# One pool of 4 KB tiles, and weight tiles that stay over several products, in a decoder trunk of fp32 matmuls

## The chip, the core and the metric

The kernel runs on one core of a Trainium2 chip. The metric is the device time of one execution in microseconds. A core has five engines that each work through a queue of their own, in order: TensorE (PE; its weight loads are listed apart as PEld), VectorE (DVE), ScalarE (ACT), GpSimd (POOL) and SyncE (SP). They wait for each other through semaphores. In this kernel SP issues nearly all plain loads from DRAM and the transposing DMAs, POOL issues the loads that add to what a tile holds, and all of them run on the core's 16 DMA engines.

## The reference, cut to what matters

Two layers over 512 positions of width 1024. Each layer is a half-weighted SwiGLU FFN, a token mixer (recurrent in layer 0, chunked spatial gating in layer 1) and a second FFN; a final RMSNorm ends it.

```python
def swiglu(x, w_in, w_out):                      # w_in 1024 x 5632, w_out 2816 x 1024
    g, u = jnp.split(x @ w_in, 2, axis=-1)
    return (jax.nn.silu(g) * u) @ w_out

for i in range(DEPTH):                           # DEPTH = 2
    h = h + 0.5 * swiglu(rms_norm(h, ffn1_norm[i]), ffn1_w_in[i], ffn1_w_out[i])
    m = recurrent_mixer(...) if i % 2 == 0 else spatial_gating_mixer(...)
    h = h + m
    h = h + 0.5 * swiglu(rms_norm(h, ffn2_norm[i]), ffn2_w_in[i], ffn2_w_out[i])
return rms_norm(h, final_norm)
```

All inputs are fp32. There are four FFNs; the change touches the output product (`@ w_out`) of the first three.

## The kernel before, in words

**Precision.** Every operand of a matmul is split into a high and a low part (`hi` by an ACT copy to the rounded type, `lo` by a DVE subtraction), and each product is three matmuls: hi·hi, lo·hi, hi·lo. The weights' parts are `whi` and `wlo`, four tiles each (pool `wp`).

**Seven products for eight.** A large product is cut into 2 x 2 blocks, A (activations) times B (weights), and done by seven block products (`seven`), in the order that the table CHAIN gives for the first three FFNs:

- P1 = A11·B11 and P2 = A12·B21
- P5 = S1·(B11+B12), P6 = S2·(B11+B12+B22), Q4 = A22·(B11+B12+B22+B21)
- P3 = S4·B22, P7 = S3·(B22+B12)

S1 to S4 are sums of blocks of A (DVE). In an output product the inner dimension of each block has six cuts: one of a single row of 128 (half a block, 256 KB) and five of two rows (512 KB). One product with one cut is a step, an entry of `subs`; a whole block's step has 12 matmuls of 128x512. CHAIN lists 42 steps: the six of P1, the six of P2, sixteen in which P5, P6 and the first four of Q4 take turns, and fourteen of P3, P7 and the last two of Q4.

**Raw weights.** `Raw` is a tile with a weight block as it is in DRAM. Its `load` issues the SP DMA (line 142), `add` the POOL DMA that adds another block to it (line 145). `Sub.split` makes whi (ACT, line 103) and wlo (DVE, line 94) from it; before that `Sub.add` may add another raw tile to it on DVE, and after the split `then` may add one more block by POOL. Of a block that is to become a sum right away (`plus`), the addition is put into POOL's queue some steps after the load (`pending`).

For one cut of an output product of the first three FFNs this gives, before the change: a load of B11 for P1 and one of B21 for P2; a second load of B11 and an addition of B12 for P5; a load of B22, which DVE adds to that tile for P6, and then an addition of B21 to it for Q4; a second load of B22 for P3, and after its split an addition of B12 for P7. That is five loads and three additions.

**The order of the work.** The program is written out step by step by the loop at the end of `trunk`; the scheduler keeps that order on each engine. At step i the loop runs the additions that are due, the hooks of phase "pre" (sums of blocks), the splits of the steps up to i+3 (`SPLIT_AHEAD`), the hooks of phases "mid" and "rest", then `load_more`, which loads raw tiles in the order of their use while fewer than `RAW_BUFS` = 8 are alive, and then the matmuls of step i. At the end of a product, DVE adds the result to the residual X (line 100), and the next norm squares it (ACT) and turns it by transposes on PE (lines 274 and 615) two or three steps later.

**Memory.** Raw tiles have a pool of their own, 8 tiles of 4 KB a partition. Everything else of this size (parts of A and their splits, partial results, planes) takes 2 KB slots from a pool of 60. A tile of a pool is free for reuse once all work on it is done, and the first write to it waits for that.

**Planes.** The result of an input product is turned into the left operand of the output product by DMA: `Group.cross` copies each tile into two planes of 16-bit halves (ACT), transposes them by DMA (SP), and merges them again (ACT, five and six steps later). `cross` handles two names (two blocks of A) at a time; both were copied and transposed in the same step, into two plane tiles and two result tiles of 2 KB.

Of the kernel before, what the change touches and what calls it, by code (L numbers as in the profile page):

```python
# [14 lines left out]
P = 128  # L15
# [17 lines left out]

RAW_BUFS = 8
SPLIT_AHEAD = 3
SLOTS = 60


KORDER = (0, 2, 4, 6, 1, 3, 5, 7)
# [20 lines left out]
def trunk(ctx: ExitStack, tc: tile.TileContext, a: dict, out: bass.AP):  # L60
    nc = tc.nc
    PS = bass.MemoryType.PSUM
    cp = ctx.enter_context(tc.tile_pool(name="cp", bufs=1))
    sp = ctx.enter_context(tc.tile_pool(name="sp", bufs=SLOTS))
    rawp = ctx.enter_context(tc.tile_pool(name="rawp", bufs=RAW_BUFS))
    wp = ctx.enter_context(tc.tile_pool(name="wp", bufs=4))
    tp = ctx.enter_context(tc.tile_pool(name="tp", bufs=8))
    mmp = ctx.enter_context(tc.tile_pool(name="mmp", bufs=6, space=PS))
# [1 line left out]
    ctx.enter_context(tc.manual_schedule())  # L70

    uid = [0]

    def nm(s):
        uid[0] += 1
        return f"{s}_{uid[0]}"

    def slot(dt=F32, name="s"):
        return sp.tile([P, T], dt, tag="s", name=nm(name))

    def bank(name="ps"):
        return mmp.tile([P, 512], F32, tag="mm", name=nm(name))
# [22 lines left out]
    def split(src):  # L105

        w = src.shape[-1]
        hi, lo = slot(F32R, "hi")[:, :w], slot(F32R, "lo")[:, :w]
        act(hi, src, AF.Copy)
        tt(lo, src, f32(hi), ALU.subtract)  # L110
        return hi, lo
# [1 line left out]

    live = set()
    pending = []
    now = [0]

    class Raw:

# [9 lines left out]

        def load(self):  # L130
            _, k, c = self.shape
            t = rawp.tile([P, 1024], F32, tag="raw", name=nm("raw"))
            self.v = t[:, : k * c].rearrange("p (k c) -> p k c", k=k)
            live.add(self)
            self.fetch()
            if self.plus is not None:
                pending.append((now[0] + self.wait, self))
                pending.sort(key=lambda p: p[0])
# [70 lines left out]
            assert self.sub.hi is not None  # L209

    raws = []

    def raw_of(src, shape, *plus):
        raws.append(Raw(src, shape, *plus))
# [40 lines left out]
    class Group:  # L255


        def __init__(self, n):
            self.n, self.f, self.hl, self.whole = n, {}, {}, False

        def new(self, name):
            self.f[name] = slot(name=name.lower())[:, : self.n * H]
            return self.f[name]

        def part(self, name, q):
# [28 lines left out]

        def direct(self, name, ps, gains):

            hi, lo = self.hl[name] = slot(F32R, "hi")[:, : self.n * H], slot(F32R, "lo")[:, : self.n * H]
            cs = [(slice(q * H, (q + 1) * H), g) for q, g in enumerate(gains)]
            for c, g in cs:
                act(hi[:, c], ps[:, c], AF.Copy, scale=g)  # L300
            for c, g in cs:
                stt(lo[:, c], ps[:, c], g, f32(hi[:, c]), ALU.mult, ALU.subtract)

        def cross(self, half, tiles, planes, merges, parts):

            w, names = 2 * self.n * P, ("A12", "A11") if half == 0 else ("S1", "A22")
            if half == 0:
                names = names[::-1]
            dt = {}

            def move():
                pl = [sp.tile([P, 2 * T], U16, tag="s", name=nm("pl"))[:, : 2 * w] for _ in tiles]
                for k, name in enumerate(names):
                    c = slice(k * w, (k + 1) * w)
                    d = dt[name] = sp.tile([P, 2 * T], U16, tag="s", name=nm("dt"))[:, : 2 * w]
                    v = d.rearrange("p (m s t) -> p m s t", s=2, t=P)
                    for s, (t, h) in enumerate(zip(pl, tiles)):
                        act(t[:, c].rearrange("p (b f) -> p b f", b=2),
                            h.bitcast(U16)[:, c].rearrange("p (f b) -> p b f", b=2), AF.Copy)
                        nc.sync.dma_start_transpose(out=v[:, :, s, :], in_=t[:, c])  # L320
                tiles.clear()
# [52 lines left out]
    def seven(block, cuts, left, w, posts, order=None, own=False, apart=False, joined=None, opening=None,  # L374
# [165 lines left out]
    class BlockNorm:  # L540


        def __init__(self, grow, plain=False, late=False, wait=()):


            self.g = [Group(2), Group(2)]
            self.grow, self.plain, self.late, self.wait = grow, plain, late, wait

        def src(self, i, name):
# [39 lines left out]
    class TileNorm:  # L589
# [29 lines left out]
        def take(self, half):  # L619
            for k in KORDER:  # L620
                ps = self.ps[k // 2][:, k % 2 * H : (k % 2 + 1) * H]
                if half == 0:
                    self.z[k] = (slot(F32R, "zh"), slot(F32R, "zl"))
# [26 lines left out]
    def out_blocks(w, k0, groups, scale, norm=None, order=None, own=False, soon={}, swap=False, p2_lag=0, chain=False):  # L650
# [934 lines left out]
    def part(i, name, q, vector=False):  # L1585

        g, c, gain = first.g[i], slice(q * H, (q + 1) * H), first.src(i, name)[1][q]
        if name not in g.hl:
            g.hl[name] = slot(F32R, "hi"), slot(F32R, "lo")
        hi, lo = (t[:, c] for t in g.hl[name])  # L1590
        src = opening[i, name][:, c]
        if vector:
# [106 lines left out]
```

## Time and profile before

| | us |
|---|---|
| median of three runs | 1603.8 (1600.93 to 1604.03) |
| the profiled execution | 1606.85 |
| its span | 1605.0 |
| PE busy in it | 1581.6 (99%) |
| DVE busy | 1315.6 (82%) |
| ACT busy | 1158.9 (72%) |

The mean granted clock of TensorE was 0.992. 275.84 MB were read from HBM.

How to read the lines: a timeline's row begins with the start and the length in us, then engine, line of the kernel, instruction, the tile written and the tiles read, shapes and the count; in brackets stands how long the engine was idle before it and what ended that. SPq, POOLq and ACTq are the queues that issue DMAs. In a table of waits a row tells who waited, for whom, how long in total, how often, and the longest of them. Matmuls are pipelined: a row of 0.39 us is followed by the next some 0.23 us later, so the pace is read from the starts.

### The profile page before, as it was taken

The numbers are of one execution on the slowest core, as the hardware profiler recorded it, in microseconds if no ns is written. First come the engines' busy times: TensorE is split into PE (matmuls) and PEld (weight loads), VectorE is DVE, ScalarE is ACT, GpSimd is POOL, SyncE is SP. The second block draws the span as 40 slices with busy tenths as digits, with TensorE's granted clock in tenths as the row PEclk, the third lists the DMA queues.
The fourth block names the chain that finished last, engine by engine and source line by source line (L and its number), as shares of the span: only waits on it lengthen the run. The fifth ranks groups of instructions, "written<-read, shape, count | busy, mean of one in ns | idle before, by whom it ended". The sixth has DMA issues, their size and how long they took to land.

```text
span 1605.0 us, 20741 instructions
## 1 busy us (share of the span) xinstructions
PE 1581.6 (99%) x7149; PEld 1304.4 (81%) x7149; DVE 1315.6 (82%) x1759; ACT 1158.9 (72%) x1696; POOL 222.5 (14%) x201
## 2 busy tenths in 40 slices
PE   9999999999999999999899999999999999999998
PEld 7788887788888888888788888887788888888886
DVE  6977777978998877778878777789878989889788
ACT  7877786558777777786567777865786775675676
POOL 2111103200010111102201111022211011111120
PEclk9999999999999999999999999999999999999999
DMA  8888779953283887779937888799888557796793
GB/s 292 182 189 192 186 213 245 202 138 97 87 213 103 178 205 193 182 222 240 209 99 182 190 193 186 211 253 200 218 199 209 158 124 194 181 221 172 174 225 100
DMA packets 247465, 299.24 MB, mean 186 GB/s; under 512 B 94672, under 2 KB 120384, under 8 KB 247360
## 3 DMA queue, kind: packets, MB, share of 16 engines
q1 hardware_dynamic: 197856, 204.78, 41.4%
q0 software_dynamic: 47712, 91.30, 33.9%
q10 hardware_dynamic: 1792, 1.84, 0.3%
q8 instruction: 56, 0.92, 0.2%
q14 instruction: 49, 0.40, 0.1%
HBM read 275.84 MB, written 2.10 MB: 173 GB/s over the span
## 4 chain that ended last, share of the span: by engine, by line
PE 79%; DMA 6%; issue 5%; DVE 4%; ACT 2%; POOL 1%; ACTq 0%; SPq 0%; POOLq 0%
PE A L421 12%; PE A L422 12%; PE A L423 12%; PE C L422 6%; PE C L423 6%; PE C L421 6%; DMA raw<-in_ffn_w_out_dram 6%; PE p L892 4%; PE B L421 3%; PE B L423 3%; PE B L422 3%; PE r L232 2%; PE r L234 2%; PE r L233 2%; PE e L274 1%
## 5 line engine op out<-in xcount | busy, mean ns | idle before, releaser
L94 DVE TENSOR_TENSOR wlo<-raw,whi 128x1024 fp32r<-128x1024 f32 (+1 forms) x537 | 639.0, 1192 | 230.6 <-ACT whi L103 228.6
L103 ACT ACTIVATE whi<-raw 128x1024 fp32r<-128x1024 f32 (+1 forms) x537 | 553.1, 1031 | 237.5 <-PE C L422 58.4
L421 PE MATMUL A<-whi,hi 128*128 128x512 f32 x1016 | 401.0, 395 | 1.9 <-ACT c L103 1.9
L422 PE MATMUL A<-whi,lo 128*128 128x512 f32 x1016 | 396.9, 391 | 0.0
L423 PE MATMUL A<-wlo,hi 128*128 128x512 f32 x1016 | 396.9, 391 | 0.0
L421 PEld LDWEIGHTS A<-whi,hi 128*128 128x128 f32 x1016 | 191.9, 189 | 46.7 <-ACT c L103 7.9
L423 PEld LDWEIGHTS A<-wlo,hi 128*128 128x128 f32 x1016 | 191.4, 188 | 40.6 <-DVE wlo L94 0.4
L422 PEld LDWEIGHTS A<-whi,lo 128*128 128x128 f32 x1016 | 191.8, 189 | 39.0 <-DVE lo L94 0.3
L422 PE MATMUL C<-whi,lo 128*128 128x512 f32 x560 | 218.9, 391 | 1.3 <-DVE lo L94 1.2
L421 PE MATMUL C<-whi,hi 128*128 128x512 f32 x560 | 218.2, 390 | 0.0
L423 PE MATMUL C<-wlo,hi 128*128 128x512 f32 x560 | 218.1, 389 | 0.0
L145 POOL DMA_DIRECT2D raw<-in_ffn_w_in_dram x82 | 99.1, 1215 | 731.4 <-ACT pl L103 312.2
L103 ACT ACTIVATE hi<-a 128x512 fp32r<-128x512 f32 (+1 forms) x188 | 111.6, 600 | 55.9 <-DVE a L94 54.3
L145 POOL DMA_DIRECT2D raw<-in_ffn_w_out_dram x72 | 83.3, 1196 | 367.4 <-DVE wlo L94 185.6
L94 DVE TENSOR_TENSOR raw<-raw,raw 128x1024 f32<-128x1024 f32 (+1 forms) x108 | 129.6, 1200 | 0.9
L422 PEld LDWEIGHTS C<-whi,lo 128*128 128x128 f32 x560 | 105.1, 188 | 25.8 <-DVE lo L94 4.1
L421 PEld LDWEIGHTS C<-whi,hi 128*128 128x128 f32 x560 | 105.2, 188 | 21.9
L94 DVE TENSOR_TENSOR lo<-a,hi 128x512 fp32r<-128x512 f32 (+1 forms) x188 | 122.0, 656 | 1.3 <-ACT hi L103 1.2
L423 PEld LDWEIGHTS C<-wlo,hi 128*128 128x128 f32 x560 | 105.1, 188 | 21.6
L422 PE MATMUL B<-whi,lo 128*128 128x512 f32 x280 | 109.1, 389 | 0.1
L421 PE MATMUL B<-whi,hi 128*128 128x512 f32 x280 | 109.0, 389 | 0.0
L423 PE MATMUL B<-wlo,hi 128*128 128x512 f32 x280 | 109.0, 389 | 0.0
(184 smaller groups left out, 2081.3 us busy)
## 6 DMA issues: line engine op xcount, KB each, us to landing
raw<-in_ffn_w_in_dram SPq DMA_DIRECT2D x161, 512.0 KB, 4.3
raw<-in_ffn_w_out_dram SPq DMA_DIRECT2D x100, 512.0 KB, 5.6
raw<-in_ffn_w_in_dram POOLq DMA_DIRECT2D x82, 512.0 KB, 7.0
raw<-in_ffn_w_out_dram POOLq DMA_DIRECT2D x60, 512.0 KB, 7.5
raw<-in_sg_w_in_dram SPq DMA_DIRECT2D x20, 512.0 KB, 6.2
raw<-in_ffn_w_in_dram SPq DMA_DIRECT2D x34, 256.0 KB, 6.5
raw<-in_rec_w_in_dram SPq DMA_DIRECT2D x16, 512.0 KB, 3.7
raw<-in_sg_w_in_dram POOLq DMA_DIRECT2D x12, 512.0 KB, 7.7
```

The lines of the kernel that those rows point to most:

```text
L94: nc.vector.tensor_tensor(out=o, in0=x, in1=y, op=op)
L103: nc.scalar.activation(out=o, in_=x, func=f, **k)
L145: nc.gpsimd.dma_start(out=self.v, in_=src, accum_op=ALU.add)
L232: nc.tensor.matmul(ps, wh, xh, start=start, stop=False)
L233: nc.tensor.matmul(ps, wh, xl, start=False, stop=False)
L234: nc.tensor.matmul(ps, wl, xh, start=False, stop=stop)
L274: nc.tensor.transpose(ps[:, o : o + P], src(q, s), ident)
L421: nc.tensor.matmul(ps, zh, wh, start=fresh and i == 0, stop=False, **k)
L422: nc.tensor.matmul(ps, zl, wh, start=False, stop=False, **k)
L423: nc.tensor.matmul(ps, zh, wl, start=False, stop=end, **k)
L892: nc.tensor.matmul(bank_of(half, s), z, (sub.lo if m == 2 else sub.hi)[:, q, :], start=left[2] == "2" and (h, q, m) == (0, 0, 0), stop=lef ...
```

## The change

The two pools become one of 38 tiles of 4 KB (`TILES`). `slot` hands out halves: the second request with the same key within four steps gets the other half of the tile. The keys pair what is used together: hi and lo of a split, A11 and A12 of a group, and so on. A raw weight tile takes a whole tile.

In the output products of the first three FFNs, the tile of P1 is kept: B12 is added to it eight steps before P5, and it goes on to P6 and Q4. The tile with B22 that P6 adds is kept for P3, and, where P7 comes four or more steps after P3 (`linked`), gets B12 added after P3's split and serves P7. The last cut, where it comes three steps after, gets a tile of its own for P7, loaded with B12 and with B22 added. So a cut has three loads and three additions, the last one four loads. From four steps before such a product to its last step but one, up to 14 raw tiles (`RAW_MORE`) may be alive.

`cross` now copies and transposes its two names in two steps that follow each other, into one 4 KB plane tile and one 4 KB result tile for both; the merges stay where they were.

```diff
-SLOTS = 60
+TILES = 38
+RAW_MORE = 14
...
-    sp = ctx.enter_context(tc.tile_pool(name="sp", bufs=SLOTS))
-    rawp = ctx.enter_context(tc.tile_pool(name="rawp", bufs=RAW_BUFS))
+    sp = ctx.enter_context(tc.tile_pool(name="sp", bufs=TILES))
...
-    def slot(dt=F32, name="s"):
-        return sp.tile([P, T], dt, tag="s", name=nm(name))
+    halves = {}
+
+    def slot(dt=F32, name="s", key=None):
+        key = (key or name, dt)
+        at, t = halves.pop(key, (None, None))
+        if t is None or now[0] > at + 4:
+            t = sp.tile([P, 2 * T], dt, tag="s", name=nm(name))
+            halves[key] = (now[0], t)
+            return t[:, :T]
+        return t[:, T:]
+
+    def hi_lo(*names):
+        key = nm("hl")
+        return [slot(F32R, name, key) for name in names or ("hi", "lo")]
...
-        hi, lo = slot(F32R, "hi")[:, :w], slot(F32R, "lo")[:, :w]
+        hi, lo = (t[:, :w] for t in hi_lo())
...
-            t = rawp.tile([P, 1024], F32, tag="raw", name=nm("raw"))
+            t = sp.tile([P, 2 * T], F32, tag="s", name=nm("raw"))
...
-            self.f[name] = slot(name=name.lower())[:, : self.n * H]
+            key = self.key(name) if self.key else (id(self), name in ("A11", "A12"))
+            self.f[name] = slot(name=name.lower(), key=key)[:, : self.n * H]
...
-            def move():
-                pl = [sp.tile([P, 2 * T], U16, tag="s", name=nm("pl"))[:, : 2 * w] for _ in tiles]
-                for k, name in enumerate(names):
...
+            def move(k, name):
+                if k == 0:
+                    dt["pl"], dt["dt"] = (sp.tile([P, 4 * T], U16, tag="s", name=nm(name)) for name in ("pl", "dt"))
...
-            hook(*planes, move)
+            for k, name in enumerate(names):
+                hook(planes[0] + k, planes[1], lambda k=k, name=name: move(k, name))
...
+        def linked(ci):
+            return order.index(("P7", ci)) - order.index(("P3", ci)) >= 4
...
             if chain:
-                if prod in ("P1", "P2"):
-                    r = new(int(prod == "P2"), 0)
+                if prod == "P1":
+                    r = raw[11, ci] = new(0, 0)
+                elif prod == "P2":
+                    r = new(1, 0)
                 elif prod == "P5":
-                    r = raw[11, ci] = new(0, 0, (0, 1))
+                    r = raw[11, ci]
+                    hook(len(subs) - 8, "pre", lambda r=r, ci=ci: r.add(block(0, 1, cuts[ci])))
                 elif prod == "P6":
                     r, tile, then = raw[11, ci], new(1, 1), block(1, 0, cuts[ci])
+                    raw[22, ci] = tile
                 elif prod == "P3":
-                    r, then = new(1, 1), block(0, 1, cuts[ci])
-                    raw[33, ci] = r
+                    r = raw[22, ci]
+                    if linked(ci):
+                        then = block(0, 1, cuts[ci])
+                elif prod == "P7" and not linked(ci):
+                    r = new(0, 1, (1, 1))
                 else:
-                    r = raw[33 if prod == "P7" else 11, ci]
+                    r = raw[22 if prod == "P7" else 11, ci]
...
+        if chain:
+            caps.append((at0 - 4, at0 + len(order) - 1))
...
-        while loaded < n and len(live) < RAW_BUFS:
+        most = RAW_MORE if any(a <= now[0] < b for a, b in caps) else RAW_BUFS
+        while loaded < n and len(live) < most:
```

More of the change, by code (lines that the diff above doesn't have):

```diff
@@ L72, in trunk @@
     uid = [0]
+    now = [0]
     def nm(s):
@@ L115, in trunk @@
     pending = []
-    now = [0]
     class Raw:
@@ L211, in trunk @@
     raws = []
+    caps = []
     def raw_of(src, shape, *plus):
@@ L258, in __init__ @@
         def __init__(self, n):
-            self.n, self.f, self.hl, self.whole = n, {}, {}, False
+            self.n, self.f, self.hl, self.whole, self.key = n, {}, {}, False, None
         def new(self, name):
-            self.f[name] = slot(name=name.lower())[:, : self.n * H]
+            key = self.key(name) if self.key else (id(self), name in ("A11", "A12"))
+            self.f[name] = slot(name=name.lower(), key=key)[:, : self.n * H]
             return self.f[name]
@@ L295, in direct @@
         def direct(self, name, ps, gains):
-            hi, lo = self.hl[name] = slot(F32R, "hi")[:, : self.n * H], slot(F32R, "lo")[:, : self.n * H]
+            hi, lo = self.hl[name] = [t[:, : self.n * H] for t in hi_lo()]
             cs = [(slice(q * H, (q + 1) * H), g) for q, g in enumerate(gains)]
@@ L309, in cross @@
             dt = {}
-            def move():
-                pl = [sp.tile([P, 2 * T], U16, tag="s", name=nm("pl"))[:, : 2 * w] for _ in tiles]
-                for k, name in enumerate(names):
[L314 to L321, printed above, removed]
+            def move(k, name):
+                if k == 0:
+                    dt["pl"], dt["dt"] = (sp.tile([P, 4 * T], U16, tag="s", name=nm(name)) for name in ("pl", "dt"))
+                c = slice(k * w, (k + 1) * w)
+                d = dt[name] = dt["dt"][:, 2 * T * k : 2 * T * k + 2 * w]
+                v = d.rearrange("p (m s t) -> p m s t", s=2, t=P)
+                for s, h in enumerate(tiles):
+                    t = dt["pl"][:, 2 * T * s + k * w : 2 * T * s + (k + 1) * w]
+                    act(t.rearrange("p (b f) -> p b f", b=2),
+                        h.bitcast(U16)[:, c].rearrange("p (f b) -> p b f", b=2), AF.Copy)
+                    nc.sync.dma_start_transpose(out=v[:, :, s, :], in_=t)
             def merge(name):
@@ L546, in __init__ @@
             self.g = [Group(2), Group(2)]
+            for g in self.g:
+                g.key = lambda name: (id(self), name)
             self.grow, self.plain, self.late, self.wait = grow, plain, late, wait
@@ L622, in take @@
                 if half == 0:
-                    self.z[k] = (slot(F32R, "zh"), slot(F32R, "zl"))
+                    self.z[k] = hi_lo("zh", "zl")
                 hi, lo = (t[:, half * H : (half + 1) * H] for t in self.z[k])
@@ L1588, in part @@
         if name not in g.hl:
-            g.hl[name] = slot(F32R, "hi"), slot(F32R, "lo")
+            g.hl[name] = hi_lo()
         hi, lo = (t[:, c] for t in g.hl[name])
```

## The prediction

> **What bounds the kernel now.** I read the page first, then the wait view, then windows over the output products, then the timelines of the places where TensorE stops.
>
> ```profile
> span 1605.0 us, 20741 instructions
> ...
> PE 1581.6 (99%) x7149; PEld 1304.4 (81%) x7149; DVE 1315.6 (82%) x1759; ACT 1158.9 (72%) x1696; POOL 222.5 (14%) x201
> ...
> raw<-in_ffn_w_out_dram SPq DMA_DIRECT2D x100, 512.0 KB, 5.6
> ...
> raw<-in_ffn_w_out_dram POOLq DMA_DIRECT2D x60, 512.0 KB, 7.5
> ```
>
> TensorE is the bound, and nothing that leaves its 7149 instructions alone can gain more than its stops. The output weights have two kinds of DMA: a plain load on SP, and on POOL a load that adds to the tile, 7.5 us to landing at the median.
>
> Windows over the three output products that the change touches (A: layer 0 first FFN, B: layer 0 second, C: layer 1 first), and over undisturbed input products:
>
> ```profile
> 225.86:344.90 119.04, 112.91 (x479) 91.56 (x478) 102.84 (x147) 78.82 (x119) 22.81 (x22) 0.96 0.88 212
> 700.87:815.79 114.92, 110.47 (x487) 90.72 (x486) 98.50 (x130) 77.76 (x118) 20.83 (x18) 0.97 0.87 217
> 1029.98:1144.24 114.26, 110.92 (x487) 90.09 (x486) 98.85 (x130) 77.38 (x119) 24.74 (x22) 0.99 0.94 229
> 850.00:950.00 100.00, 100.00 (x440) 82.03 (x439) 73.23 (x77) 75.97 (x99) 12.07 (x10) 1.00 0.83 196
> ```
>
> Columns: length, busy time and count of PE, PEld, DVE, ACT, POOL, the granted clock, the DMA share, GB/s. In the input products PE is busy all of the time at clock 1.00. The output products lose clock and PE time, with DMA at 0.87 to 0.94 and DVE above 98 us. How much each loses follows from the clean pace:
>
> ```profile
> 785.38 0.39 PE L421 MATMUL C<-whi,hi 128*128 128x512 f32 x1
> ...
> 788.10 0.39 PE L421 MATMUL A<-whi,hi 128*128 128x512 f32 x1
> ...
> 734.87 1.04 PE L274 MATMUL e<-ident,x 128*128 128x128 f32 x8
> ```
>
> From 785.38 to 788.10 lies one step of 12 matmuls: 2.72 us, 0.2267 each. An output product has 7 products of 5 whole blocks (12 matmuls) and one half block (6): 462 matmuls, 104.7 us. The norm's transposes inside it cost 0.8 us per eight (the next matmul starts at 735.67): 2.4 us in B and C (24), 1.6 in A (16). So A loses 119.0 - 104.7 - 1.6 = 12.7 us, B 114.9 - 107.1 = 7.8, C 114.3 - 107.1 = 7.2: 27.7 us in all. This is the most that the change can win there.
>
> **What the stops wait for.** In B:
>
> ```profile
> 788.53 1.20 POOL L145 DMA_DIRECT2D raw<-in_ffn_w_out_dram  x1 [3.47 <-DVE wlo L94]
> ...
> 796.97 1.06 ACT L103 ACTIVATE whi<-raw 128x1024 fp32r<-128x1024 f32 x1 [4.54 <-DMA raw<-in_ffn_w_out_dram]
> ...
> 798.06 1.23 DVE L94 TENSOR_TENSOR wlo<-raw,whi 128x1024 fp32r<-128x1024 f32 x1 [3.95 <-ACT whi L103]
> ...
> 799.80 1.28 DVE L100 SCALAR_TENSOR_TENSOR x<-C,x 128x512 f32<-128x512 f32 x2
> ...
> 800.55 2.35 PE L274 MATMUL e<-ident,x 128*128 128x128 f32 x8 [4.12 <-DVE x L100]
> ```
>
> The last block's P3 is split, POOL adds B12 to that tile for P7 only three steps later, 8.4 us pass, ACT waits 4.54 us for it, DVE's update of x stands behind that split in its queue, and PE stands 4.12 us for x. In A and C:
>
> ```profile
> 262.41 1.20 POOL L145 DMA_DIRECT2D raw<-in_ffn_w_out_dram  x1 [1.58 <-DVE wlo L94]
> 272.97 2.44 POOL L145 DMA_DIRECT2D raw<-in_ffn_w_out_dram  x2 [9.36 <-DMA raw<-in_ffn_w_out_dram]
> ...
> 273.79 2.00 ACT L103 ACTIVATE whi<-raw 128x1024 fp32r<-128x1024 f32 x2 [3.54 <-DMA raw<-in_ffn_w_out_dram]
> 283.38 1.06 ACT L103 ACTIVATE whi<-raw 128x1024 fp32r<-128x1024 f32 x1 [2.01 <-DMA raw<-in_ffn_w_out_dram]
> ...
> 274.90 0.50 PE L421 MATMUL Q<-whi,hi 128*128 128x512 f32 x1 [1.27 <-ACT whi L103]
> 327.34 1.06 ACT L103 ACTIVATE whi<-raw 128x1024 fp32r<-128x1024 f32 x1 [2.84 <-DMA raw<-in_ffn_w_out_dram]
> ...
> 332.06 3.25 PE L615 MATMUL xt<-ident,xn 128*128 128x128 f32 x14 [3.17 <-ACT xn L103]
> ...
> 1093.72 1.06 ACT L103 ACTIVATE whi<-raw 128x1024 fp32r<-128x1024 f32 x1 [3.32 <-DMA raw<-in_ffn_w_out_dram]
> ...
> 1128.73 2.01 ACT L103 ACTIVATE whi<-raw 128x1024 fp32r<-128x1024 f32 x2 [0.67 <-DMA raw<-in_ffn_w_out_dram]
> ...
> 1129.44 0.33 PE L274 MATMUL e<-ident,x 128*128 128x128 f32 x1 [1.93 <-DVE x L100]
> ```
>
> The addition issued at 262.41 feeds Q4 at 273.79, 11.4 us later. The next stood ready on POOL behind one that waited 9.36 us for a plain load (P5's own B11, to which POOL adds B12): POOL issues in order, so a late load holds up the additions for Q4. Over the whole run:
>
> ```profile
> ACT whi L103 <- DMA raw<-in_ffn_w_out_dram: 35.5, 16, 4.5
> POOL raw L145 <- DMA raw<-in_ffn_w_out_dram: 126.1, 12, 37.1
> ```
>
> **The change, part by part.**
>
> *Loads.* Per block five plain loads become three (B11 of P5 and B22 of P3 go; the last block gets one B12 back for P7): 30 become 19 in each of A, B, C, 33 fewer of 390 on SP. POOL's 189 issues stay in number, PE, DVE and ACT run the same instructions in the same order except for one move below. In A, B, C this takes 11 loads of some 512 KB from 48 transfers. POOL's additions then wait for a tile that landed long ago, so the 9.36 us hold-up has no cause left; a late load would next be late for P1 or P2 alone. P5's addition is now ordered 8 steps ahead of its product, which is split 3 steps ahead: of 5 steps (13.6 us) the addition takes 7.5, so 6.1 us are spare if P1's split frees the tile late.
>
> *The last block's P7.* It no longer waits for P3 of three steps before; its load and addition go out early. That removes 4.54 us of ACT's wait in B and 2.84 in A. What is late next in B: ACT is free at 792.4 (796.97 less 4.54), whi takes 1.06, wlo 1.2 and a left part 0.7, so x is updated from about 796.0 instead of 799.80, and PE, done at 796.4 (800.55 less 4.12), waits about 0.7 us instead of 4.1. In A:
>
> ```profile
> 325.57 1.28 DVE L100 SCALAR_TENSOR_TENSOR x<-C,x 128x512 f32<-128x512 f32 x2
> ...
> 328.31 0.61 ACT L103 ACTIVATE junk<-x 128x512 f32<-128x512 f32 x1
> ```
>
> The squares (junk) waited behind that whi. Started at 326.9, when x is done, they bring the transposes of 332.06 forward by 1.5 us; PE was done at 328.9, so I keep 1.7 us of 3.17. In C the addition of the second last block (four steps, 10.9 us) still stands before x; I keep 0.8 of 1.93.
>
> *Half clock.* After a stop the next matmuls run slower:
>
> ```profile
> 277.30 0.63 PE L423 MATMUL Q<-wlo,hi 128*128 128x512 f32 x1
> 277.72 0.63 PE L421 MATMUL Q<-whi,hi 128*128 128x512 f32 x1
> ```
>
> They start 0.42 us apart instead of 0.227; some eight do, 1.6 us. This followed a stop of only 1.27 us here, and the window 225.86:344.90 has its clock at 0.96; it is part of the 27.7 us. A stop of 1.9 us in the input products was not followed by it:
>
> ```profile
> PE A L421 <- ACT c L103: 1.9, 1, 1.9
> ...
> 50.00:100.00 50.00, 48.12 (x213) 39.48 (x212) 40.76 (x57) 42.20 (x61) 5.99 (x5) 1.00 0.94 216
> ```
>
> So I count no half clock behind stops under 1 us. The Trainium skill (TensorE: Matmul & The Clock Gate, Part 1) has the clock fall only after a whole idle window of about 3.4 us. The stop of 1.27 us disagrees with it; by that rule the slow matmuls there have another cause, which is rival 5.
>
> *One pool.* 60 x 2 KB and 8 x 4 KB are as many bytes as 38 x 4 KB. A tile is free when both halves are, so buffers come back later; but a load takes any free tile and no longer the one of eight. SP's waits today:
>
> ```profile
> SPq L142 <- DVE wlo L94: 716.9, 237, 16.8
> SPq L320 <- ACT pl L103: 169.4, 54, 21.7
> ```
>
> The first is the small raw pool. I followed SP's new queue along this timeline, each issue behind its predecessor and behind the trace's end of what it waits for: with 5.6 us for a load, 7.5 for an addition, 2.5 for a transpose, no plain load reaches its reader with less than 5 us spare after the opening, and only eight additions miss theirs, by up to 1.1 us: the same eight, by as much, that miss it when today's queue is laid out so. Bound: 0 to 3 us; I take 0.5 for each of A, B, C. Free tiles also let the loads of the next product run further ahead, into the end of the input products (DMA share 0.8 there): bounded by the same figure.
>
> *The planes.* The copies and transposes of a block's second name go out one step later, its merge stays. ACT's 0.6 us copies merely change places. A step is 2.72 us and the second name's merge still comes five steps after its copies, 13.6 us for two transposes behind each other, against 2.5 us for one:
>
> ```profile
> dt<-pl SPq DMA_TRANSPOSE x168, 2.5
> ```
>
>  It spreads SP's transposes, a gain that I put at nothing.
>
> *Sum.* A: 12.7 less 1.7 kept, less 1.3 for slower matmuls behind that stop, less 0.7 for waits for a left half that come from DVE itself: 9.0. B: 7.8 - 1.0 = 6.8. C: 7.2 - 1.2 = 6.0. Together 21.8, less 1.5 for the pool: 20.3 us. The profiled execution took 1606.85 us, which gives 1586.5. The median of the runs shown, 1603.8, is 3.0 us lower; the forecast on it is 1584.
>
> **Rivals.** (1) The additions stay slow. They go on reading and writing 512 KB on the same DMA engines as SP's prefetch, which now may have 14 tiles open. Q4 follows P6 by four or five steps (10.9 us at least, less the split's 2.3), so at the 11.4 us of 262.41 to 273.79 the Q4 stops stay; only the P7 part and POOL's hold-up go. A keeps 6 of its 12.7 us, B 2.5, C 4.5: 13 us kept, 14.7 won, less 1.5: 1590 to 1591. For it: the 11.4 us; against: 783.85 below took at most 6.2 us. The Trainium skill (DMA: Bandwidth & Descriptors, Queues, rings and completion order) says each engine takes turns between the queues, packet by packet. By that, an addition is slowed as long as SP's queue holds anything, however many loads were dropped, which is this rival; the 6.2 us, inside the stretch of rival 2 with its DMA share of 1.03, do not bear it out.
>
> ```profile
> 783.85 1.20 POOL L145 DMA_DIRECT2D raw<-in_ffn_w_out_dram  x1 [4.99 <-DVE wlo L94]
> ...
> 790.01 1.04 ACT L103 ACTIVATE whi<-raw 128x1024 fp32r<-128x1024 f32 x1
> ```
>
> (2) DVE becomes the bound of the second half of the product:
>
> ```profile
> 781.00:794.00 13.00, 13.00 (x60) 10.74 (x58) 13.00 (x18) 7.41 (x10) 2.41 (x2) 1.00 1.03 234
> ```
>
> It is busy all 13 us, and PE too: DVE holds the pace without any reserve. If it enters this half as late as now, each of the three transitions keeps about what C's lost with the least wait for DMA (1.93 us with 0.67): 6 us more, 1590.
>
> (3) Slower: SP issues in order, and a load that gets a tile whose second half is still read holds the transposes behind it; the merge, on ACT in order, then holds PE at the next block. There are 18 FFN input chunks in the three FFNs. It decides from 1.1 us in each (20 us over 18); at 2 us each the time is 1620. Against: the spare time found above.
>
> (4) Nothing: the loads that go were prefetched and hidden anyway, the late ones are additions, whose number stays. Then 1602 to 1605. Against: the 126.1 us in which POOL waits for such loads.
>
> (5) The slow matmuls behind the shorter stops, in A at 277 and in C behind 1129.44, have another cause than the stop and stay: 2 x 1.6 us, 1587. Against: they begin right behind the stop.
>
> **How the numbers follow.** Forecast 0.61; rival 1 0.17, rival 2 0.10, rival 3 0.04, rival 4 0.04, rival 5 0.04. Anything within 0.2% (3.2 us) is no change that a measurement of this kernel can tell. Faster 0.92 (the forecast, rivals 1, 2 and 5), same 0.04 (rival 4), slower 0.04 (rival 3). The range: below, the gain is at most 27.7 us, of which 26 gives 1578; above, rivals 1 and 2 together, 1590.5 and 6, 1596.
>
> **What would show it.** The window of B falls from 114.9 to about 108 us with PE busy and clock 1.00; ACT's wait for DMA of the output weights from 35.5 to under 10 us; POOL's wait for loads of them from 126.1 to under 20; PE's 4.12 us before the transposes of x to under 1; SP's 512 KB loads of output weights from 100 to 73. Wrong would be: new PE stops inside input products (rival 3), ACT still waiting for DMA at Q4 (rival 1), or no ACT waits but PE waiting for DVE's left halves (rival 2).

## The result and the profile after

The changed kernel takes 1640.9 us at the median (1638.9 to 1651.6), beside 1602.4 for the kernel before on the same chip: a ratio of 1.0256, 95% interval 1.0209 to 1.0303. It is slower by 2.6%, where 1.2% faster was forecast. The profiled execution took 1640.34 us.

Lines of the page after: the span, the engines' busy time, and the DMA issues with their size and median us from issue to landing; the transposes are from the view of the DMAs.

```profile
span 1638.6 us, 20627 instructions
...
PE 1589.0 (97%) x7149; PEld 1308.6 (80%) x7149; DVE 1316.5 (80%) x1759; ACT 1156.1 (71%) x1696; POOL 223.1 (14%) x201
...
raw<-in_ffn_w_in_dram SPq DMA_DIRECT2D x161, 512.0 KB, 8.0
raw<-in_ffn_w_in_dram POOLq DMA_DIRECT2D x82, 512.0 KB, 10.2
raw<-in_ffn_w_out_dram SPq DMA_DIRECT2D x73, 512.0 KB, 10.5
raw<-in_ffn_w_out_dram POOLq DMA_DIRECT2D x60, 512.0 KB, 8.5
```

```profile
dt<-pl SPq DMA_TRANSPOSE x168, 3.7
```

The five compute rows of the page count as many instructions as before. The loads of the output weights fell from 100 to 73, as the change says. But at the median each kind takes longer to land: a plain load of output weights 10.5 us instead of 5.6, an addition 8.5 instead of 7.5, a transpose 3.7 instead of 2.5.

The same three output products A, B and C in windows (length; busy time and count of PE, PEld, DVE, ACT and POOL; granted clock, DMA share, GB/s):

```profile
233.46:351.26 117.80, 110.70 (x480) 90.08 (x478) 99.71 (x143) 77.11 (x116) 20.54 (x20) 0.97 0.85 193
715.10:834.08 118.98, 110.72 (x487) 90.66 (x486) 97.68 (x129) 77.65 (x119) 18.62 (x16) 0.97 0.79 187
1048.66:1175.17 126.51, 113.87 (x487) 92.74 (x486) 98.81 (x130) 77.86 (x119) 27.91 (x24) 0.95 0.92 212
```

Before they took 119.0, 114.9 and 114.3 us. Instead of 21.8 us less, they take 15.1 us more; the other 18.5 us that the profiled execution lost lie outside them. The waits after, with total us, times and longest:

```profile
ACT whi L117 <- DMA raw<-in_ffn_w_in_dram: 44.8, 21, 3.2
POOL raw L158 <- DMA raw<-in_ffn_w_out_dram: 35.9, 7, 15.6
ACT a L117 <- DMA dt<-pl: 26.8, 3, 9.4
ACT whi L117 <- DMA raw<-in_ffn_w_out_dram: 18.1, 9, 5.0
PE A L437 <- ACT hi L117: 15.8, 3, 6.1
PE e L289 <- DVE x L114: 7.3, 3, 5.1
```

SP's own waits after:

```profile
SPq L336 <- ACT pl L117: 430.2, 55, 36.4
SPq L155 <- DVE wlo L108: 177.8, 41, 32.5
SPq L155 <- DMA dt<-pl: 47.6, 12, 9.3
```

The waits that the change was to shorten did fall: POOL's for plain loads from 126.1 to 35.9 us, ACT's for output weights from 35.5 to 18.1. New ones stand beside them: ACT waits 44.8 us for input weights and 26.8 us, in three pieces, for transposed planes. And SP no longer waits 716.9 us for DVE's splits before a load, but 177.8; it waits 430.2 us for the planes' copies instead of 169.4. Loads still wait for tiles, but now also for tiles that other work used last: 47.6 us until transposes have landed, for example.

One of the three long waits, at the head of A, in the timeline (start, us, engine; three queues, one after the other):

```profile
223.39 2.50 SPq L336 DMA_TRANSPOSE dt<-pl  x2
225.93 4.12 SPq L155 DMA_DIRECT2D raw<-in_ffn_w_out_dram  x7
230.14 7.76 SPq L336 DMA_TRANSPOSE dt<-pl  x1
...
246.41 1.17 ACT L117 ACTIVATE a<-dt 128x1024 uint16<-128x1024 uint16 x1 [8.09 <-DMA dt<-pl]
...
250.13 0.50 PE L437 MATMUL A<-whi,hi 128*128 128x512 f32 x1 [4.28 <-ACT hi L117]
```

The limit on open weight tiles rises from 8 to 14 four steps ahead of the product. At that step SP has just sent the transposes of a block's first name. It then sends seven loads within 4.12 us, none of which waits more than 0.4 us for a tile, and only behind them the second name's transposes, which go out one step later since the change. ACT reaches their merge at 238.3 and stands 8.09 us; the left parts behind it come late, and PE stands.

### The profile page after: what moved, and what is told of

Read it like the earlier page. It is cut to its first block, busy times and chain, and to the rows that moved or that the text cites. A ratio compares the mean times of both kernels' runs of the same rounds, so it can differ in the third digit from the quotient of the medians.

```text
span 1638.6 us, 20627 instructions
## 1 busy us (share of the span) xinstructions
PE 1589.0 (97%) x7149; PEld 1308.6 (80%) x7149; DVE 1316.5 (80%) x1759; ACT 1156.1 (71%) x1696; POOL 223.1 (14%) x201
## 5 line engine op out<-in xcount | busy, mean ns | idle before, releaser
L437 PE MATMUL A<-whi,hi 128*128 128x512 f32 x1016 | 405.7, 399 | 27.7 <-ACT hi L117 15.8
L438 PE MATMUL A<-whi,hi 128*128 128x512 f32 x1016 | 402.1, 396 | 2.8 <-DVE hi L108 2.8
L439 PE MATMUL A<-wlo,hi 128*128 128x512 f32 x1016 | 401.0, 395 | 0.4 <-DVE wlo L108 0.4
L437 PEld LDWEIGHTS A<-whi,hi 128*128 128x128 f32 x1016 | 194.3, 191 | 75.5 <-ACT c L117 18.5
L438 PEld LDWEIGHTS A<-whi,hi 128*128 128x128 f32 x1016 | 194.3, 191 | 44.1 <-DVE hi L108 4.8
L437 PE MATMUL C<-whi,hi 128*128 128x512 f32 x560 | 218.2, 390 | 0.0
L438 PE MATMUL C<-whi,hi 128*128 128x512 f32 x560 | 218.0, 389 | 0.1
L117 ACT ACTIVATE hi<-a 128x512 fp32r<-128x512 f32 (+1 forms) x177 | 106.0, 604 | 54.9 <-DVE a L108 50.0
L438 PEld LDWEIGHTS C<-whi,hi 128*128 128x128 f32 x560 | 105.1, 188 | 22.4 <-DVE hi L108 0.7
L437 PEld LDWEIGHTS C<-whi,hi 128*128 128x128 f32 x560 | 105.1, 188 | 21.8
L439 PEld LDWEIGHTS C<-wlo,hi 128*128 128x128 f32 x560 | 105.1, 188 | 21.8
L108 DVE TENSOR_TENSOR hi<-a,hi 128x512 fp32r<-128x512 f32 (+1 forms) x177 | 116.1, 662 | 1.3 <-ACT hi L117 1.2
L438 PE MATMUL B<-whi,hi 128*128 128x512 f32 x280 | 109.3, 390 | 0.0
L437 PE MATMUL B<-whi,hi 128*128 128x512 f32 x280 | 109.3, 390 | 0.0
## 6 DMA issues: line engine op xcount, KB each, us to landing
raw<-in_ffn_w_out_dram SPq DMA_DIRECT2D x73, 512.0 KB, 10.5
```

The source lines that it names most:

```text
L108: nc.vector.tensor_tensor(out=o, in0=x, in1=y, op=op)
L117: nc.scalar.activation(out=o, in_=x, func=f, **k)
L437: nc.tensor.matmul(ps, zh, wh, start=fresh and i == 0, stop=False, **k)
L438: nc.tensor.matmul(ps, zl, wh, start=False, stop=False, **k)
L439: nc.tensor.matmul(ps, zh, wl, start=False, stop=end, **k)
```

## The experiments

Four theories. T1: the raise of the limit sends a burst of loads ahead of transposes. T2: the pool takes away what paced SP everywhere; with eight buffers each load waited for the split of the tile eight loads earlier. T3: the second name's later step is what lets loads pass in front of its transposes. T4: tiles that come free only when both halves are free hold the engines up. Each comparison is with the kernel before on the same chip (medians 1603.4 to 1604.8).

**The raise, six steps later.**

```diff
-            caps.append((at0 - 4, at0 + len(order) - 1))
+            caps.append((at0 + 2, at0 + len(order) - 1))
```

> The changed kernel, with the raise of the limit from 8 to 14 open weight tiles put off by six steps (from four steps ahead of each output product to two steps into it), past the last transposes of the input product before it. Theory T1 (burst: at the raise SP issues seven loads of 512 KB between the transposes of a block's first and second name; the second name's land behind 3.5 MB, its merge stops ACT, ACT stops PE): the three stops of 8.35, 8.88 and 9.53 us at the head of the output products fall under 2 us each, their slow matmuls go too, and the time falls from 1641 to 1600-1612 us. Theory T2 (one pool lets SP run ahead of the transposes in every stage, whatever the limit): the stops at 67, 226, 708 and 1159 us stay and the time stays at 1630-1640 us. Theory T4 (tiles that come free in halves only hold SP): nothing changes, 1638-1641 us.

Measured: 1626.0 us, ratio 1.012 (1.0092 to 1.0147), between the ranges of T1 and T2. The burst at the heads is some 15 of the 38 us, so T1 alone falls. ACT's wait for a transposed `a` is gone from the list; its wait for input weights is not:

```profile
ACT whi L117 <- DMA raw<-in_ffn_w_in_dram: 49.9, 23, 4.0
```

**Both names in one step again.**

```diff
-                hook(planes[0] + k, planes[1], lambda k=k, name=name: move(k, name))
+                hook(*planes, lambda k=k, name=name: move(k, name))
```

> The changed kernel, with the copies and transposes of a block's second name back in the step of the first, as in the kernel before; limit, pool and kept tiles as changed. T1 with the moved name as the second condition (T3: the loads pass only because the second name goes out a step later): the transposes stand ahead of the seven loads on SP, the stops of 8.35, 8.88 and 9.53 us go, 1600-1612 us. T1 without it (the burst slows transposes by sharing the DMA engines, wherever they stand in the queue): stops of 4 us and more stay, 1620-1641 us. T2: 1630-1640 us.

Measured: 1609.0 us, ratio 1.0021 (1.0006 to 1.0036). With this line alone 32 us come back. T3 holds as a condition; but the saved loads still win nothing.

**The second name later, in the kernel before.** Two pools and before's loads; `move` is called once for each name, the second one step later, as in the change.

> The kernel before, two pools and its own loads, with one thing changed: the copies and transposes of a block's second name go out one step later. T1: nothing pushes seven loads in between, 1600-1606 us. T3 (a step between the two names is by itself enough for loads to get in front of the second): PE stops of 3 us and more before the merges of the second name, 1612-1640 us.

Measured: 1606.7 us, ratio 1.0005 (0.9987 to 1.0024): no difference. A later step by itself costs nothing; it needs the pool. The transposes take 3.6 us to landing here, as long as in the changed kernel (3.7), so that figure comes with the later step and is no loss by itself.

**The pool without kept tiles or raise.** As changed, with before's loads in the three output products and no `caps`.

> The changed kernel with the loads of the three output products as in the kernel before (five plain loads per block, nothing kept) and no raise of the limit; the pool of 38 tiles and the moved second name stay. T1: no burst, so no stop above 5 us at the heads of the output products, and the output products as slow as before: 1600-1612 us. T2 and T4 (the pool by itself does it): 1625-1645 us.

Measured: 1635.3 us, ratio 1.0177 (1.0155 to 1.02). T1 said 1600 to 1612: there is no burst from a raise here, and 31 us are lost all the same. What the pool does to SP shows in its wait for splits:

```profile
SPq L155 <- DVE wlo L108: 157.6, 48, 18.1
```

At the end of the input product ahead of B, the issues of 18 us (672 to 690; median us to landing) and the timeline of SP, ACT and PE:

```profile
raw<-in_ffn_w_in_dram POOLq DMA_DIRECT2D x4, 512.0 KB, 14.7
raw<-in_ffn_w_out_dram SPq DMA_DIRECT2D x4, 512.0 KB, 17.6
```

```profile
676.10 3.51 SPq L336 DMA_TRANSPOSE dt<-pl  x2
679.66 2.57 SPq L155 DMA_DIRECT2D raw<-in_ffn_w_out_dram  x3
...
692.96 1.18 ACT L117 ACTIVATE s<-dt 128x1024 uint16<-128x1024 uint16 x1 [4.89 <-DMA dt<-pl]
702.01 1.06 ACT L117 ACTIVATE whi<-raw 128x1024 fp32r<-128x1024 f32 x1 [2.90 <-DMA raw<-in_ffn_w_in_dram]
705.88 1.05 ACT L117 ACTIVATE c<-A 128x512 f32<-128x512 f32 x2
706.50 0.77 PE L437 MATMUL A<-whi,hi 128*128 128x512 f32 x1 [3.88 <-ACT c L117]
```

The loads here are for B and are first read some 30 us later. Three of them go out within 2.57 us, as soon as SP gets past its transposes; the loads take 17.6 us at the median, and the four additions to input weights that are needed now take 14.7. ACT waits 4.89 us for a transposed part and then for an addition; this part's transposes were issued ahead of the three loads (both were out by 679.61), so it was not a place behind this burst that made them late. After that the eviction `c` is late, and PE stops.

**Eight buffers of their own.** The version just shown, with one thing changed:

```diff
-TILES = 38
+TILES = 30
...
+    rawp = ctx.enter_context(tc.tile_pool(name="rawp", bufs=8))
...
-            t = sp.tile([P, 2 * T], F32, tag="s", name=nm("raw"))
+            t = rawp.tile([P, 2 * T], F32, tag="raw", name=nm("raw"))
```

> The version with the pool alone (before's loads, no raise, the second name a step later: 1635 us), with the weight tiles back in eight buffers of their own and 30 tiles of 4 KB, handed out in halves, for everything else. Theory T2 (the eight buffers paced SP: each load waited for the split of the tile eight loads earlier; in the one pool a free tile is always there, three to seven loads go out within 2 us each, and additions and transposes issued behind them land 15 to 20 us later): SP's wait for DVE's splits is back near 700 us, the 512 KB loads of input weights land in some 4.5 us instead of 8.0, additions in 7 to 8 instead of 11.2, and the time is 1600-1608 us. Theory T4 (halves of a tile that come free together hold SP or the engines): still 1625-1637 us.

Measured: 1606.2 us, ratio 1.0017 (0.9998 to 1.0036). All but a few us of the 31 are back, with the 30 remaining tiles still handed out in halves: T4 falls for these tiles. This run undoes two things at once, the missing pacing and the sharing of tiles between weights and the rest. The rows are of an execution of 1616.0 us, the slowest of its ten. SP's wait, then the loads of input weights of the whole run, the issues of the same 18 us of the program (670.2 to 688.2) and SP's timeline in it:

```profile
SPq L156 <- DVE wlo L109: 717.6, 233, 16.8
```

```profile
raw<-in_ffn_w_in_dram SPq DMA_DIRECT2D x161, 512.0 KB, 4.6
```

```profile
raw<-in_ffn_w_in_dram POOLq DMA_DIRECT2D x4, 512.0 KB, 10.7
raw<-in_ffn_w_out_dram SPq DMA_DIRECT2D x3, 512.0 KB, 7.7
```

```profile
674.28 3.24 SPq L337 DMA_TRANSPOSE dt<-pl  x2
684.55 3.35 SPq L156 DMA_DIRECT2D raw<-in_ffn_w_out_dram  x2
```

Behind the transposes the next load now waits until 684.55, two loads lie 3 us apart, and the additions take 10.7 us instead of 14.7. ACT's wait for the same transposed part is 1.40 us instead of 4.89.

**The pool alone.** Before's loads, no raise, both names in one step.

> One pool, before's loads, no raise of the limit, and both names' transposes in one step as before: the pool with nothing else. If the unpaced loads cost only together with the moved second name: 1602-1610 us, with loads of input weights still at 7 to 8 us. If the unpaced loads cost by themselves: 1615-1635 us.

Measured: 1615.2 us, ratio 1.0075 (1.0052 to 1.0098). The pool costs 12 us by itself, and 20 more with the second name later. In the profiled executions, which lie 6 us apart, the loss is in the output products: together they take 355.3 us instead of 348.2, and plain loads of their weights take 10.9 us to landing instead of 5.6. ACT's wait for input weights tells the two apart: 8.7 us here, 36.3 in the version with the second name later, and 9.6 with eight buffers and the second name later. Here and there:

```profile
ACT whi L117 <- DMA raw<-in_ffn_w_in_dram: 8.7, 5, 2.9
```

```profile
ACT whi L117 <- DMA raw<-in_ffn_w_in_dram: 36.3, 20, 3.0
```

```profile
ACT whi L118 <- DMA raw<-in_ffn_w_in_dram: 9.6, 6, 2.9
```

**The raise, only as long as it serves.** One pool, kept tiles, both names in one step. All 19 loads of an output product are out by its step 7; what the limit of 14 lets in after that belongs to the next product.

```diff
-            caps.append((at0 - 4, at0 + len(order) - 1))
+            caps.append((at0 - 4, at0 + 8))
```

> One pool, kept tiles, both names' transposes in one step (1609 us with the limit of 14 up to the product's end), with the limit of 14 from four steps ahead to step 8 only; by step 7 all 19 loads of the product are out, and the loads of the next product then wait until fewer than 8 tiles are open, some 24 steps later. If the prefetch of the next product is what slows the additions and takes back the gain in the output products: additions of output weights land in 5 to 7 us instead of 8.9, the last product loses nothing any more at its end (it lost 5.4 us), and the time is 1590-1600 us. If the additions are slow by themselves (rival 1): 1605-1611 us.

Measured: 1595.0 us, ratio 0.9945 (0.9927 to 0.9964), 14 us less than with the raise up to the product's end. But the additions of output weights still take 8.1 us, against 8.9 with the long raise and 5 to 7 expected: only a part of their slowness goes. The third output product, and ACT's wait for the output weights, with the long raise and then with the short one:

```profile
1026.91:1146.54 119.63, 112.58 (x488) 91.03 (x486) 99.23 (x130) 77.15 (x119) 27.43 (x24) 0.97 0.97 226
```

```profile
ACT whi L117 <- DMA raw<-in_ffn_w_out_dram: 26.6, 13, 4.9
```

```profile
1020.81:1134.28 113.47, 110.67 (x487) 91.34 (x486) 99.33 (x130) 77.26 (x119) 26.30 (x22) 0.97 0.94 222
```

```profile
ACT whi L117 <- DMA raw<-in_ffn_w_out_dram: 14.6, 8, 3.8
```

**Kept tiles with paced loads.** Both names in one step, ten weight buffers of their own, 28 tiles for the rest, and a limit of ten throughout.

```diff
-RAW_BUFS = 8
-TILES = 38
-RAW_MORE = 14
+RAW_BUFS = 10
+TILES = 28
+RAW_MORE = 10
...
+    rawp = ctx.enter_context(tc.tile_pool(name="rawp", bufs=10))
...
-            t = sp.tile([P, 2 * T], F32, tag="s", name=nm("raw"))
+            t = rawp.tile([P, 2 * T], F32, tag="raw", name=nm("raw"))
...
-                hook(planes[0] + k, planes[1], lambda k=k, name=name: move(k, name))
+                hook(*planes, lambda k=k, name=name: move(k, name))
```

> Kept tiles and both names' transposes in one step, with ten buffers for weights alone (limit 10 throughout) and 28 tiles of 4 KB in halves for the rest: the saved loads with SP still paced by the buffers. T2: loads land in some 4.5 to 6 us, the output products keep 10 to 20 us of the forecast gain, 1586-1598 us. If ten tiles leave the loads of the products late, or if the gain was never there: 1600-1612 us.

Measured: 1583.2 us (1582.6 to 1584.2), ratio 0.9878 (0.9863 to 0.9893), a little below the range expected. This version beats both kernels. The windows of its output products, the additions to output weights, ACT's wait for output weights and SP's for splits:

```profile
226.66:334.97 108.31, 106.81 (x479) 88.27 (x478) 100.34 (x144) 77.05 (x117) 20.71 (x20) 1.00 0.82 179
691.05:798.47 107.42, 107.42 (x487) 89.22 (x486) 98.56 (x130) 77.90 (x119) 18.75 (x16) 1.00 0.84 182
1012.68:1120.10 107.42, 107.42 (x487) 89.20 (x486) 98.55 (x130) 77.32 (x119) 24.94 (x21) 1.00 0.92 192
```

```profile
raw<-in_ffn_w_out_dram POOLq DMA_DIRECT2D x60, 512.0 KB, 7.4
```

```profile
ACT whi L118 <- DMA raw<-in_ffn_w_out_dram: 8.0, 6, 2.6
```

```profile
SPq L156 <- DVE wlo L109: 724.5, 233, 16.8
```

In B and C PE is busy in every microsecond, at clock 1.00. How much of this comes from the kept tiles and how much from two more buffers is not shown: no run has before's five loads with ten buffers and a limit of ten.

**The same, with the second name later.**

> Kept tiles in ten weight buffers (1583 us), with the second name's copies and transposes a step later, as in the change. If that move costs only where the loads are not paced: 1582-1586 us. If it costs by itself: 1590 us and more.

Measured: 1583.3 us, ratio 0.9871 (0.9856 to 0.9886). With paced loads the moved name costs nothing here either.

**Slack in the buffers.** Two runs on before's loads, second name later, eight open tiles at most: ten weight buffers and 28 tiles, and 13 buffers and 25 tiles.

> The version with eight weight buffers of their own and 30 other tiles (1606 us), with ten weight buffers and 28 other tiles, while the program still opens at most eight weight tiles: before's loads, the second name a step later. Two buffers of slack, so a load waits for the split of the tile ten loads earlier instead of eight. T2 (what costs is that SP's loads are no longer paced): between 1606 and 1635 us, with SP's wait for DVE's splits between 180 and 700 us and loads of input weights between 4.6 and 8.0 us. If sharing, not pacing, is the cause: 1603-1610 us. 28 tiles by themselves cost nothing (1583 us with ten buffers and kept tiles).

Measured: 1613.6 us, ratio 1.0056 (1.0034 to 1.0078). SP's wait for splits and the issues lie between those of eight buffers and those of the one pool, as T2 asks:

```profile
SPq L156 <- DVE wlo L109: 587.6, 187, 16.8
```

```profile
raw<-in_ffn_w_in_dram SPq DMA_DIRECT2D x161, 512.0 KB, 6.4
raw<-in_ffn_w_in_dram POOLq DMA_DIRECT2D x82, 512.0 KB, 10.1
```

The time agrees in sign, but its interval just touches that of eight buffers (up to 1.0036), and 28 tiles instead of 30 are a second change, so it weighs little. ACT's wait for input weights is 40.8 us here (in an execution of 1623.5 us, the slowest of seven), more than the 36.3 in the one pool with the second name later, although the median is 22 us lower. So that wait is a sign of the slower additions, not a measure of the loss.

> As the version with eight weight buffers of their own (before's loads, the second name a step later: 1606 us), with one number changed: 13 weight buffers (and 25 other tiles for 30), while the program's order still opens no more than eight tiles at a time. A load then meets a buffer that came free five loads earlier and does not wait. T2 (the pacing by the eight buffers is what was lost, not anything of sharing): SP's wait for DVE's splits falls from some 700 to under 250 us, loads of input weights go from 4.6 to 7 us and more, the time to 1620-1637 us. If the sharing of the pool itself cost (loads waiting for tiles of planes and parts): 1602-1610 us.

Measured: 1659.0 us, ratio 1.0337 (1.0315 to 1.036): more than any theory gave. The 25 tiles were a second change in this run, as the next two show.

> Kept tiles and both names' transposes in one step, with 13 weight buffers, 25 other tiles and a limit of 13 throughout. Here buffers and limit are equal, so each load waits for the split of the tile 13 loads earlier: paced, though from further ahead. T2: as with ten, 1581-1588 us. If it is the depth of the prefetch that slows the additions and transposes, rather than the bursts: 1592-1610 us.

Measured: 1635.9 us, ratio 1.0203 (1.0187 to 1.022), against 1581 to 1588 by T2. The range of the other theory, 1592 to 1610, is missed as well. Its loads are fast (4.6 us for input weights), its stops are others.

> As the version with eight weight buffers of their own and 30 other tiles (1606 us), with 25 other tiles; five tiles stay unused. Theory T5 (25 tiles are too few for planes, parts and blocks: an eviction waits for a tile that transposes still read or write, ACT and TensorE stand 6 us and more at 190, 663 and 993 us, as in the version with 13 weight buffers): stops of 6 us and more at these places, loads of input weights still at some 4.6 us, 1625-1645 us; then of the 53 us between 8 buffers with 30 tiles and 13 buffers with 25 some 30 come from the tiles and some 20 from the loads. If 25 tiles do: 1604-1610 us, and all 53 us come from the loads.

Measured: 1649.0 us, ratio 1.0265 (1.0238 to 1.0292). Eight buffers, paced loads, and 25 tiles alone cost 43 us, a little above T5's range. There an eviction has no tile until transposes have landed:

```profile
PE A L438 <- ACT c L118: 34.7, 4, 12.1
ACT c L118 <- DMA dt<-pl: 24.9, 3, 9.0
```

So of the 53 us between eight buffers with 30 tiles and 13 buffers with 25, some 43 come from the tiles and 10 from the slack. These 10 us are the cleanest case for T2: the weights have buffers of their own in both runs, only the number of these differs (8 and 13), and the intervals lie apart. Loads of input weights go from 4.4 to 7.0 us, and ACT's wait for input weights from 3.8 to 31.5. The two waits of T5 stand in the run with kept tiles in 13 buffers as well (23.3 and 16.2 us); whether a deeper prefetch costs anything by itself stays open.

## Why the prediction was wrong

The loss adds up along four steps, by the medians (measured on different chips, on which the kernel before took 1602.4 to 1604.8): the pool alone 1603.4 to 1615.2 (+12), kept tiles with the short raise to 1595.0 (-20), the raise up to the product's end to 1609.0 (+14), the second name one step later to 1640.9 (+32). The forecast had 1.5, -21.8, nothing beyond the 1.5, and nothing for these.

**The gain in A, B and C: right in size, in another kernel.** Forecast were 9.0, 6.8 and 6.0 us off 119.0, 114.9 and 114.3, which leaves 110.0, 108.1 and 108.3. With the loads paced they take 108.3, 107.4 and 107.4. ACT's wait for output weights was to fall under 10 us and is 8.0; PE's waits for `x` ahead of the norm's transposes, up to 5.1 us in the changed kernel, are gone from the list. POOL's wait for plain loads was to fall under 20 us; it is 40.6 there and 35.9 in the changed kernel. That the version's 1583.2 us lies so near the forecast 1584 is partly luck: it has ten buffers, a limit of ten and no common pool, and its windows win 25.1 us where 21.8 were forecast. In the changed kernel as it stands the windows show nothing of the gain.

**"One pool": wrong, and here the forecast failed.** I laid out SP's new queue with "5.6 us for a load, 7.5 for an addition, 2.5 for a transpose" and concluded that the pool costs 0 to 3 us. These durations came from a trace in which eight buffers kept the loads apart. They are not properties of a load: the same 512 KB of input weights take 4.6 us at the median with eight buffers and 8.0 in the one pool. I had quoted SP's 716.9 us for DVE's splits and given them no use; they kept the loads apart. And the term names no addition to input weights, where ACT now waits 44.8 us instead of 4.7. Measured, the pool alone costs 12 us.

**Loads that run further ahead, "bounded by the same figure", 0 to 3 us: wrong.** The raise lasts through the whole product, so 14 tiles are filled for the next product while additions for this one are due: 14 us. A second effect of the raise is the seven loads at its start. I took the limit of 14 from the diff and did not ask at which step it rises and what is next in SP's queue there.

**"The planes": wrong in the pool.** I put the move at nothing, "13.6 us for two transposes behind each other, against 2.5 us for one". It is nothing with paced loads (ratio 1.0005; 1583.3 against 1583.2). In the one pool it costs 20 us with before's loads and 32 in the change, the largest single term. At the heads of the output products the seven loads go out between the two names; what makes up the other part is not settled.

**The half clock: right as far as seen.** With the stops gone, all three windows of the version with ten buffers show clock 1.00: rival 5's slow matmuls went with the stops.

**The rivals.** Rival 1 is part of what happened: with 14 tiles open for the next product the additions of output weights took 8.9 us and ACT waited 26.6 us for them. I gave it 0.17, with one addition of 6.2 us against it. Rival 2 falls: with ten buffers PE is busy 107.42 of 107.42 us in B, its second half included, without waiting for DVE. Rival 3 named the place and the path, transposes on SP behind loads, late merges, PE, but not the cause. Loads in the pool do wait for tiles that transposes or matmuls used last (47.6 us for transposes above), but hardly in front of a transpose: in the changed kernel's trace such waits hold back transposes whose copies are ready by some 5 us in all. At the heads of the output products the loads hardly waited at all (0.4 us at most). Rival 3's 1620 us got a chance of 0.04, because the durations that spoke against it were the paced ones.

What stays open: eight buffers of their own give back 29 us. With no tile shared, slack takes 10 us of them (five more buffers, clear of the noise) or some 7 (two more buffers, barely); so much is shown for the pacing. SP's waits and the landing times move with the rest, but whether the other 20 us or so are pacing too, or the sharing of tiles, no run separates.

## What to carry to other kernels

A small buffer pool can also be a throttle: before it is enlarged or merged, see what its release held back, and what shares the DMA engines with it. Durations of DMAs from a trace hold for the traffic of that trace; when a change alters when loads are issued, cost the urgent transfers behind a burst, not alone. When tiles are to stay longer, give them just the buffers they need and keep the wait that paces the rest: here ten weight buffers of their own beside 28 tiles for the rest, with a limit of ten, turned a loss of 2.6% into a gain of 1.2%. Too few tiles for the rest cost as much as the pool did: five fewer cost 43 us.

## What the runs showed of the hardware

SP was held up in issuing, not only its DMAs in landing: a pair of transposes goes out in 2.50 us at 223.39, while one of the same kind behind seven loads took 7.76 us until the next could go. The Trainium skill (DMA: Bandwidth & Descriptors, Queues, rings and completion order) has each DMA engine take one queue's descriptors in ring order and take turns between queues. The order agrees with the transposes that landed only behind the seven loads. The turns would have the additions on POOL's queue slowed by a burst on SP's, not stopped: 14.7 against 10.7 us above agrees. How the engines share packet by packet no run here shows.

But a burst alone does not do it. With the pool alone, all four transposes going first, the same 18 us (662.3 to 680.3) have five such loads, and the additions are as fast as with eight buffers:

```profile
raw<-in_ffn_w_out_dram SPq DMA_DIRECT2D x5, 512.0 KB, 15.8
raw<-in_ffn_w_in_dram POOLq DMA_DIRECT2D x4, 512.0 KB, 10.8
```

I had not expected that the place of two transposes matters to additions; why it does, these runs do not settle.
